# One more seven-product tile in the second FFN, a later start of the down weights in the first, and a down weight made between two copies

## The chip, the cores and the metric

One core of one Trainium2 chip runs the whole layer. The time is device microseconds (us) of one execution, the median over runs. The profile is of one execution, taken by the hardware profiler; its lines name instructions by engine (PE the matrix engine, PEld its weight loads, DVE the vector engine, ACT the scalar engine, POOL and SP the two engines that issue the DMAs here) and by the line of the kernel (L1021).

## The reference

A decoder layer on 512 tokens of width 1024 in float32: a SwiGLU feed-forward block (FFN1), a mixer (attention beside a recurrence), and a second SwiGLU block (FFN2), each between two RMS norms. The change touches the two feed-forward blocks only:

```python
def swiglu(x, w_gate, w_up, w_down):
    return (jax.nn.silu(x @ w_gate) * (x @ w_up)) @ w_down

f = swiglu(rms_norm(h, ffn1_norm_pre[l]), ffn1_w_gate[l], ffn1_w_up[l], ffn1_w_down[l])
h = h + 0.5 * rms_norm(f, ffn1_norm_post[l])
...
f = swiglu(rms_norm(h, ffn2_norm_pre[l]), ffn2_w_gate[l], ffn2_w_up[l], ffn2_w_down[l])
h = h + 0.5 * rms_norm(f, ffn2_norm_post[l])
```

The hidden width is 2816, which is 22 tiles of 128. Weights arrive in float32.

## The kernel before, in words

**Arithmetic.** Every float32 operand is split into a high and a low part (`split`: ACT copies the source to the high part at L269, DVE subtracts that from the source at L270), and a product is three matmuls: high by high, high by low, low by high. A split of 128x1024 is thus one ACT and one DVE instruction, and both engines work nearly all the time to make the operands that PE consumes.

**The hidden tiles of an FFN** are made one after another, in the order that `ffn_order` writes out. The first `NSTD[n]` of them (6 in FFN1, 4 in FFN2) are standard: a gate and an up product, 24 matmuls of 128x512 each. All further tiles are "seven-product" tiles (a Strassen scheme over the two halves of the input width and of the tokens, gate and up sharing products): seven products p1 to p7 of 12 matmuls of 128x256, in the order p1, p5, p6, p2, p7, p3, p4 (`prod`, L994; its matmuls are L1008 to L1010). Their weights are made in `w_forms_in_place` (L646) from one raw load of 1 MB, in four splits that the text calls a (for p1, p2), d (p4), c (p7, p5) and b (p6, p3), with four DVE additions between them (L654, L655, L657, L658). The input must be there in seven forms as well, each one a split (`x_forms` in FFN1, `forms_of` in FFN2, recorded a step at a time after the standard tiles).

Within a seven-product tile, ACT takes the bank of p1 to another bank (L1029, the Y copy; p6 adds to the emptied bank, so it waits for it), then copies the results of p5 and p6 out of their banks (`copy`, L1016: c5 and c6). After p7 a DVE sum (`sum_of`, L1021) forms one half of u from p7's bank and c5. p4 is written into that same bank, so **p4 waits for this sum**. Another sum after p3 forms half of g; two SiLUs and two DVE products (L1049, L1050) end the tile.

**The down projection** is interleaved with the hidden tiles: the first 16 hidden tiles, taken four at a time, are multiplied by their down weights in seven products as well (`step`, L913, 24 matmuls of 128x512 at L922 to L924). They sit in "windows" between a tile's products and its finish. `WINDOWS` gives the steps of four consecutive tiles: p1 and p2, then p5, then p6 and p7, then p3 and p4. In FFN1 the windows of tiles 7 to 12 are written out in `LEAD`. A step's weight is made ahead by `down_form` (L897): a split of 128x1024 from `dr0`, `dr1` or `npair`, SBUF tiles that POOL fills by DMA (L879, or L881 where the load adds to what is there); once made, it issues the load of the next weight into the same place (`supply`, L885), and POOL's DMA waits for the DVE half of the split to be done with the source. The weights that the coming window needs are the tile's `due` list. In the kernel before, all of them are recorded after p2 "behind" the last copy, c6 (`behind("copy")`: in the list order not before it). Tiles with two dues are i = 1, 3 and 4 of each four (p1 and p2; p6 and p7; p3 and p4), tiles with one due are those ahead of p5.

**The start of the down weights.** `begin` (L907) copies one column of `ub` into `dr0` and `dr1` on DVE (L909). The copy reads a hidden tile just made, so the two first POOL loads into `dr0` and `dr1` cannot start before that tile is there: it is a gate in time, and the copied values are overwritten by the loads. `begin` is called after standard tile 1 of each FFN.

**Order.** A scheduler places each engine's instructions in one fixed list at build time, from the recorded order and priorities; each engine then runs its list from top to bottom. Raw weights come through two SBUF buffers, loaded by SP (L215); split weights through four buffers of 128x2x1024.

Of the kernel before, what the change touches and what calls it, by code (L numbers as in the profile page):

```python
# [18 lines left out]
D = 1024  # L19
KC = D // P  # L20
NF = 22
NSTD = {1: 6, 2: 4}
SEVEN = 4
STEPS = ("p1", "p2", "p5", "p6", "p7", "p3", "p4")
WINDOWS = (("p1", "p2"), ("p5",), ("p6", "p7"), ("p3", "p4"))
# [2 lines left out]
LAST = (16, 22)  # L28
# [26 lines left out]
def ffn_order(n):  # L55

    n0 = NSTD[n]
    order = [("std", f) for f in range(n0)]
# [96 lines left out]
def hybrid_layer(ctx: ExitStack, tc: tile.TileContext, xT: bass.AP, xN: bass.AP, wst: bass.AP,  # L155
                 first: bass.AP, rows: bass.AP, wdn: bass.AP, wbig: bass.AP, consts: bass.AP, bias: bass.AP, out: bass.AP):
    nc = tc.nc
    DVE, ACT, PE = nc.vector, nc.scalar, nc.tensor
# [109 lines left out]
    def split(dh, dl, src):  # L268
        ACT.activation(dh, src, AF.Copy)  # L269
        DVE.tensor_sub(dl, src, dh.bitcast(F32))  # L270
# [9 lines left out]
    def tmp(name):  # L280
        return tpool.tile([P, T], F32, name=name, tag="t")
# [534 lines left out]
    def ffn(n, x, r, forms_x, home, pss):  # L816
        t, steps = forms_x
        n0 = NSTD[n]
        ub, wdt, dr = home.ub, home.wd, home.dr
# [50 lines left out]
        def last_act(f):  # L870
            v = home.slot((f - LAST[0] - 1) % 8)
            return v[:, 0, :], v[:, 1, :]
# [12 lines left out]
        def supply(a, p):  # L885

            if p in ("p5", "p6", "p3"):
                dst, qs = home.x, {"p5": ("u0", "u1"), "p6": ("g0",), "p3": ("g1",)}[p]
            else:
                dst, qs = dr[p in ("p2", "p4")], {"p1": ("g0",), "p2": ("g1",), "p7": ("u0", "g0"), "p4": ("u1",)}[p]  # L890
            for i, q in enumerate(qs):
                load(dst, a, q, i > 0 or p in ("p6", "p3"))
            at[p] = dst
# [3 lines left out]
        def down_form(a, p):  # L897
            w = wdt[home.n % 2]
            home.n += 1
            split(w[:, 0, :], w[:, 1, :], at[p])  # L900
            ready[p] = w
            q = NEXT[p]
            a += p in ("p7", "p3", "p4")
            if a < SEVEN:
                supply(a, q)

        def begin():  # L907
            for i in range(2):
                DVE.tensor_copy(dr[i][:, 0:1], ub[:, 1, 0:1])  # L909
            for p in ("p1", "p2"):  # L910
                supply(0, p)

# [73 lines left out]
        @contextmanager  # L986
        def behind(*engines):
            with ExitStack() as es:
                for e in engines:
                    if e in last:  # L990
                        es.enter_context(tc.issue_after(last[e]))
                yield

        def prod(f, w, due):  # L994

            g = tmp("g")
            b, y, z = b_of[f % 2][:, :HB], y_[:, :HB], z_[:, :HB]
            u = ub[:, f % 4, :] if 4 < f < LAST[0] else tmp("u")
            if n == 1 and f in (6, 8):
                u = tmp("u")  # L1000

            def product(p, ps, start):
                if len(t[p][0].shape) == 4:
                    ps = ps.rearrange("q (b t) -> q b t", b=2)
                for k in range(4):
                    ks = slice(k * P, (k + 1) * P)
                    wh, wl, xh, xl = w[p][:, 0, ks], w[p][:, 1, ks], t[p][0][:, k], t[p][1][:, k]
                    PE.matmul(ps, wh, xh, start=start and k == 0, stop=False, skip_group_check=True)  # L1008
                    PE.matmul(ps, wh, xl, start=False, stop=False, skip_group_check=True)  # L1009
                    i = PE.matmul(ps, wl, xh, start=False, stop=k == 3, skip_group_check=True)  # L1010
                last["PE"] = i.ins

            def copy(ps):
                c = tpool.tile([P, HB], F32, name="c", tag="c", bufs=CB)
                with tc.high_priority(offset=EVAC):
                    last["copy"] = ACT.activation(c, ps, AF.Copy).ins  # L1016
                return c

            def sum_of(dst, ps, c):
                with tc.high_priority(offset=EVAC):  # L1020
                    DVE.tensor_add(dst, ps, c)  # L1021

            lead = f == n0
            with behind("PE"):
                product("p1", b, True)
            c1 = copy(b) if lead else None
            if not lead:
                with tc.high_priority(offset=EVAC):
                    ACT.activation(y, b, AF.Copy)  # L1029
            product("p5", z, True)  # L1030
            c5 = copy(z)
            product("p6", b, False)
            c6 = copy(b)
            product("p2", y, lead)
            if lead:
                sum_of(g[:, lo_], y, c1)
            with behind("copy"):
                for a, p in due:
                    down_form(a, p)
            product("p7", b, False)  # L1040
            sum_of(u[:, hi_], b, c5)
            with tc.high_priority(offset=EVAC):
                ACT.activation(g[:, lo_], g[:, lo_] if lead else y, AF.Silu)
            product("p3", z, False)
            sum_of(g[:, hi_], z, c6)
            product("p4", b, False)
            last["ACT"] = ACT.activation(g[:, hi_], g[:, hi_], AF.Silu).ins
            with tc.high_priority(offset=EVAC):
                DVE.scalar_tensor_tensor(u[:, lo_], g[:, lo_], -1.0, b, op0=ALU.mult, op1=ALU.mult)  # L1049
            last["DVE"] = DVE.scalar_tensor_tensor(u[:, hi_], g[:, hi_], -1.0, u[:, hi_], op0=ALU.mult,  # L1050
                                                   op1=ALU.mult).ins
            return u

        def finish(f, u):

            if f >= LAST[0]:
                split(*last_act(f), u)
                if f == LAST[0]:
                    fourth_forms()
            elif n == 1 and f < 10:  # L1060
                if f == 6:
                    second_forms()
                    third_forms()
                    fourth_forms()
                    ACT.activation(ub[:, 0:2, :], late(), AF.Copy)
                    ACT.activation(ub[:, 2, :], u, AF.Copy)
                elif f == 7:
                    first_forms()
                elif f == 8:
                    second_forms()  # L1070
                    third_forms()
                    ACT.activation(ub[:, 0, :], u, AF.Copy)
                elif f == 9:
                    fourth_forms()
            elif f % 4 == 2:
                first_forms()
            elif f % 4 == 3:
                second_forms()
                third_forms()
            elif f % 4 == 0 and f > 4:  # L1080
                fourth_forms()
# [12 lines left out]
        for at_, ev in enumerate(order):  # L1094
            if ev[0] == "std":
                j = ev[1]
                while len(pss) < 2 * j + 2:
                    pss.append(acc_ps())
                    gemm(pss[-1], fetch(keys[len(pss) - 1]), x)
                u = std_out(pss[2 * j], pss[2 * j + 1], j)  # L1100
                if j < len(steps):
                    steps[j]()
                if j == 1:
                    begin()
                if j + 1 == n0:
                    supply(0, "p5")
                    for f in steps[n0:]:
                        f()
                    if n0 > 4:
                        first_forms()  # L1110
            elif ev[0] == "prep":
                with behind("DVE", "ACT"):
                    forms[ev[1]] = w_forms_in_place(("gu", n, ev[1]))
            elif ev[0] == "prod":
                due = order[at_ + 1]
                u = prod(ev[1], forms.pop(ev[1]), [(due[1], p) for p in due[2][:2]] if due[0] == "window" else [])
                if ev[1] == 4:
                    part0(u)
            elif ev[0] == "finish":
                finish(ev[1], u)  # L1120
            else:
                for i, p in enumerate(ev[2]):
                    with behind("PE"):
                        step(ev[1], p)
                    if len(ev[2]) > 2 and i == 0:
                        down_form(ev[1], ev[2][2])
# [56 lines left out]
    with ExitStack() as mx:  # L1183
# [221 lines left out]
        for c in range(0, KC, 2):  # L1405
            g, u = tmp("g"), tmp("u")
# [6 lines left out]
        for i, (c, kind) in enumerate(AHEAD_PAIRS):  # L1413
            g, u = tmp("g"), tmp("u")
# [5 lines left out]
            f = AF.Sigmoid if kind == "sig" else AF.Gelu_apprx_tanh  # L1420
# [7 lines left out]
    with ExitStack() as mx:  # L1428
# [159 lines left out]
        for c in range(KC):  # L1588
# [16 lines left out]
                 {(1, 3): lambda: (bd2.turn(0), bd2.turn(1))})  # L1605
    keys = [(w, 2, i) for i in range(NSTD[2]) for w in ("gate", "up")]
    pss = gemm_first(keys[:NFIRST], u2, [home2.spare()[2]],
# [137 lines left out]
```

## Time and profile before

| | |
|---|---|
| median of 3 runs | 1224.08 us (1223.52 to 1226.09) |
| the profiled execution | 1225.99 us, of which the span of its instructions is 1224.1 us |
| PE busy | 1211.3 us (99%) |
| DVE busy | 979.2 us (80%) |
| ACT busy | 742.8 us (61%) |
| chain of waits that ended last | PE 85%, DVE 8%, DMA 3%, issue 2%, ACT 1% |
| matmuls recorded | 7754 |

A PE row's own duration (0.28 or 0.39 us) overlaps that of the next, since matmuls are pipelined; what counts for the time is the distance from one start to the next. A row of the timeline gives the start in us from the span's beginning, the duration, the engine, the line, the operation, out<-in, the shape, and in brackets the idle time before it with what ended that, where there was any.

### The profile page before, as it was taken

To read this page: it belongs to the slowest core of one execution; us is meant where nothing else is said; L and a number is where in the kernel's file an instruction comes from. 1 tells how busy PE (TensorE), PEld (TensorE's weight loads), DVE (VectorE), ACT (ScalarE), POOL (GpSimd) and SP (SyncE) were. 2 spreads that over 40 slices of the span, in tenths; PEclk is the share of its full clock that TensorE was granted. 3 is DMA by queue.
4 is the path that set the end of the run, shared out by engine and by line. 5 is a ranking of instruction groups with operands and counts; after the bars stand their busy time and mean duration, and the time that the engine had idled before them with its cause. 6 is when DMAs were issued, how large, how long until landed. Compare 5 with 4: busy or idle time off the path is not lost.

```text
span 1224.1 us, 19485 instructions
## 1 busy us (share of the span) xinstructions
PE 1211.3 (99%) x7754; PEld 1100.6 (90%) x7754; DVE 979.2 (80%) x1531; ACT 742.8 (61%) x1232; POOL 84.3 (7%) x139
## 2 busy tenths in 40 slices
PE   9999999999999999999999999999999999999998
PEld 7888989999878899999999888888899999999996
DVE  7899778888579897898776998755689887979864
ACT  6457665655556565665666788634556665656552
POOL 0001101010102000000001000000110010101000
PEclk9999999999999999999999999999999999999999
DMA  7336546464735322222235223524463555555441
GB/s 246 138 104 171 158 111 168 134 165 116 258 134 155 114 94 102 81 79 82 92 138 182 94 86 125 203 83 165 139 199 106 157 158 147 156 139 163 114 155 69
DMA packets 37451, 167.63 MB, mean 137 GB/s; under 512 B 4208, under 2 KB 7664, under 8 KB 25328
## 3 DMA queue, kind: packets, MB, share of 16 engines
q1 hardware_dynamic: 18432, 107.13, 25.3%
q0 software_dynamic: 18928, 59.25, 18.3%
q8 instruction: 61, 1.00, 0.3%
q14 instruction: 30, 0.25, 0.1%
HBM read 153.79 MB, written 8.39 MB: 132 GB/s over the span
## 4 chain that ended last, share of the span: by engine, by line
PE 85%; DVE 8%; DMA 3%; issue 2%; ACT 1%; POOL 0%; SPq 0%; DVEq 0%; ACTq 0%; POOLq 0%
PE bank L1008 9%; PE bank L1009 8%; PE bank L1010 8%; PE bank L675 6%; PE bank L676 6%; PE bank L677 6%; PE bank L284 6%; PE bank L285 6%; PE bank L286 6%; PE bank L923 4%; PE bank L922 4%; PE bank L924 4%; PE bank L405 3%; PE bank L404 3%; PE bank L406 3%
## 5 line engine op out<-in xcount | busy, mean ns | idle before, releaser
L270 DVE TENSOR_TENSOR w<-raw,w 128x1024 fp32r<-128x1024 f32 (+1 forms) x274 | 298.9, 1101 | 63.5 <-ACT w L269 57.8
L269 ACT ACTIVATE w<-raw 128x1024 fp32r<-128x1024 f32 (+1 forms) x274 | 256.8, 956 | 103.1 <-PE bank L286 41.4
L1008 PE MATMUL bank<-big,w 128*128 128x256 f32 x816 | 233.9, 287 | 4.5 <-DVE g L837 1.3
L1009 PE MATMUL bank<-big,w 128*128 128x256 f32 x816 | 230.8, 283 | 0.0
L1010 PE MATMUL bank<-big,w 128*128 128x256 f32 x816 | 229.4, 283 | 0.0
L1008 PEld LDWEIGHTS bank<-big,w 128*128 128x128 f32 x816 | 156.2, 191 | 10.0 <-DVE u L1021 2.0
L1009 PEld LDWEIGHTS bank<-big,w 128*128 128x128 f32 x816 | 156.4, 192 | 1.5
L1010 PEld LDWEIGHTS bank<-big,w 128*128 128x128 f32 x816 | 155.8, 192 | 0.0
L922 PE MATMUL bank<-wd,act 128*128 128x512 f32 x224 | 87.8, 392 | 0.0
L923 PE MATMUL bank<-wd,act 128*128 128x512 f32 x224 | 87.8, 392 | 0.0
L924 PE MATMUL bank<-wd,act 128*128 128x512 f32 x224 | 87.2, 389 | 0.0
L675 PE MATMUL bank<-big,w 128*128 128x256 f32 x252 | 73.0, 290 | 0.0
L677 PE MATMUL bank<-big,w 128*128 128x256 f32 x252 | 71.5, 284 | 0.0
L676 PE MATMUL bank<-big,w 128*128 128x256 f32 x252 | 71.2, 283 | 0.0
L285 PE MATMUL bank<-act,w 128*128 128x512 f32 (+1 forms) x184 | 64.8, 353 | 0.1
L286 PE MATMUL bank<-act,w 128*128 128x512 f32 (+1 forms) x184 | 64.7, 352 | 0.0
L284 PE MATMUL bank<-act,w 128*128 128x512 f32 (+1 forms) x184 | 64.5, 355 | 0.2 <-ACT act L361 0.2
L1016 ACT ACTIVATE c<-bank 128x256 f32<-128x256 f32 x70 | 26.7, 383 | 61.1 <-PE bank L1010 60.7
L270 DVE TENSOR_TENSOR wd<-npair,wd 128x1024 fp32r<-128x1024 f32 x24 | 29.4, 1224 | 39.2 <-ACT wd L269 39.2
L284 PE MATMUL bank<-big,w 128*128 128x512 f32 x144 | 56.0, 389 | 0.0
L285 PE MATMUL bank<-big,w 128*128 128x512 f32 x144 | 56.0, 389 | 0.0
L286 PE MATMUL bank<-big,w 128*128 128x512 f32 x144 | 56.0, 389 | 0.0
(399 smaller groups left out, 3206.3 us busy)
## 6 DMA issues: line engine op xcount, KB each, us to landing
raw<-in_w SPq DMA_DIRECT2D x90, 1024.0 KB, 5.0
dr<-in_wdn POOLq DMA_DIRECT2D x40, 512.0 KB, 5.2
npair<-in_wdn POOLq DMA_DIRECT2D x32, 512.0 KB, 5.5
big<-act POOLq DMA_DIRECT2D x6, 512.0 KB, 3.8
h<-in_x SPq DMA_DIRECT2D x8, 256.0 KB, 5.2
h<-in_xn POOLq DMA_DIRECT2D x4, 512.0 KB, 5.2
raw<-in_wbig SPq DMA_DIRECT2D x2, 1024.0 KB, 4.8
kept_m<-h POOLq DMA_DIRECT2D x4, 512.0 KB, 2.9
```

The costliest lines, as they stand in the source:

```text
L269: ACT.activation(dh, src, AF.Copy)
L270: DVE.tensor_sub(dl, src, dh.bitcast(F32))
L284: PE.matmul(ps, wh, xh, start=first, stop=False)
L285: PE.matmul(ps, wh, xl, start=False, stop=False)
L286: PE.matmul(ps, wl, xh, start=False, stop=last)
L675: PE.matmul(ps, wh, xh, start=start and k == 0, stop=False, skip_group_check=True)
L676: PE.matmul(ps, wh, xl, start=False, stop=False, skip_group_check=True)
L677: PE.matmul(ps, wl, xh, start=False, stop=k == 3, skip_group_check=True)
L922: PE.matmul(ps, xh, wh, start=start and k == 0, stop=False, skip_group_check=True)
L1008: PE.matmul(ps, wh, xh, start=start and k == 0, stop=False, skip_group_check=True)
L1009: PE.matmul(ps, wh, xl, start=False, stop=False, skip_group_check=True)
L1010: i = PE.matmul(ps, wl, xh, start=False, stop=k == 3, skip_group_check=True)
```

## The change

Three edits.

1. `NSTD[2]` goes from 4 to 3: hidden tile 3 of FFN2 becomes a seven-product tile. Its u goes to `ub[:, 3]` like that of the standard tiles before it, and `finish` makes no forms at tile 3 (`part0` at tile 4 makes all of them, as before). The steps that make the input's forms and the start of the p5 down weight follow standard tile 2 in place of tile 3.
2. `begin` takes the tile: in FFN1 it is called after standard tile 2 and reads `ub[:, 2]`; in FFN2 it stays after tile 1.
3. In `prod`, all dues but the last are recorded after c5, behind it, so between c5 and c6; only the last stays behind c6. Nothing changes in tiles with one due. This holds in both FFNs.

```diff
-NSTD = {1: 6, 2: 4}
+NSTD = {1: 6, 2: 3}
...
-        def begin():
+        def begin(j):
             for i in range(2):
-                DVE.tensor_copy(dr[i][:, 0:1], ub[:, 1, 0:1])
+                DVE.tensor_copy(dr[i][:, 0:1], ub[:, j, 0:1])
...
-            u = ub[:, f % 4, :] if 4 < f < LAST[0] else tmp("u")
+            u = ub[:, f % 4, :] if 4 < f < LAST[0] or f < 4 else tmp("u")
...
             product("p5", z, True)
             c5 = copy(z)
+            with behind("copy"):
+                for a, p in due[:len(due) - 1]:
+                    down_form(a, p)
             product("p6", b, False)
             c6 = copy(b)
...
             with behind("copy"):
-                for a, p in due:
+                for a, p in due[len(due) - 1:]:
                     down_form(a, p)
...
-            elif f % 4 == 3:
+            elif f % 4 == 3 and f > 4:
...
-                if j == 1:
-                    begin()
+                if j == (2 if n == 1 else 1):
+                    begin(j)
```

Where the instructions go. First DVE near the start of FFN1, before the change; `h`, `t1`, `t2` and `big` belong to the input's forms, `w8` are weight splits, L837 to L840 are the ends of standard tiles, L909 is the gate:

```order
L523 TENSOR_TENSOR t1_325<-h_93 128x1024
L909 COPY dr0_100<-ub_97 128x1
L909 COPY dr1_101<-ub_97 128x1
L270 TENSOR_TENSOR w8_471<-raw_469,w8_471 128x1024
L270 TENSOR_TENSOR w8_498<-raw_469,w8_498 128x1024
L837 TENSOR_TENSOR g_387<-bank4_77,npair_95 128x512
L839 TENSOR_TENSOR ub_97<-bank0_73,npair_95 128x512
```

And after it, further on in the same list:

```order
L839 TENSOR_TENSOR ub_97<-bank0_73,npair_95 128x512
L527 SCALAR_TENSOR_TENSOR t2_388<-h_94,t1_325 128x1024
L840 TENSOR_TENSOR ub_97<-ub_97,g_383 128x512
L270 TENSOR_TENSOR big_390<-t1_325,big_390 128x1024
L541 TENSOR_TENSOR h_93<-h_94,h_93 128x4x256
L909 COPY dr0_100<-ub_97 128x1
L909 COPY dr1_101<-ub_97 128x1
L270 TENSOR_TENSOR w8_536<-raw_534,w8_536 128x1024
```

The two copies moved eight rows down; the rows between them are otherwise in the same order.

Second, DVE in FFN2, tile 7, which has two dues (`wd1` from `npair` for p6, `wd0` from `dr0` for p7). Before:

```order
L658 TENSOR_TENSOR raw_9180<-raw_9180 128x512
L270 TENSOR_TENSOR wd1_7929<-npair_95,wd1_7929 128x1024
L270 TENSOR_TENSOR wd0_7928<-dr0_7930,wd0_7928 128x1024
L1021 TENSOR_TENSOR ub_7927<-bank1_74,c_9224 128x256
L270 TENSOR_TENSOR w8_9184<-raw_9180,w8_9184 128x1024
L1021 TENSOR_TENSOR g_9198<-bank5_78,c_9238 128x256
```

After:

```order
L658 TENSOR_TENSOR raw_9235<-raw_9235 128x512
L270 TENSOR_TENSOR wd1_7929<-npair_95,wd1_7929 128x1024
L270 TENSOR_TENSOR wd0_7928<-dr0_7930,wd0_7928 128x1024
L270 TENSOR_TENSOR w8_9239<-raw_9235,w8_9239 128x1024
L1021 TENSOR_TENSOR ub_7927<-bank1_74,c_9279 128x256
L270 TENSOR_TENSOR w8_9238<-raw_9235,w8_9238 128x1024
```

The split c of the next tile's weights now stands ahead of the sum for which p4 waits. The same swap stands in tiles 8, 9, 10, 13, 15, 17, 19 and 20 of FFN1 and in tiles 8, 9, 11, 13, 15, 17, 19 and 20 of FFN2. Tiles with one due had the order w8, then sum, before the change already.

Third, ACT in FFN1, tile 11 (window p6 and p7). Before:

```order
L934 ACTIVATE s5_873<-bank7_80 128x512
L1029 ACTIVATE bank2_75<-bank1_74 128x256
L1016 ACTIVATE c_1469<-bank1_74 128x256
L269 ACTIVATE w8_1415<-raw_1411 128x1024
L269 ACTIVATE wd0_98<-npair_95 128x1024
```

After:

```order
L934 ACTIVATE s5_873<-bank7_80 128x512
L269 ACTIVATE wd0_98<-npair_95 128x1024
L1029 ACTIVATE bank2_75<-bank1_74 128x256
L1016 ACTIVATE c_1472<-bank1_74 128x256
L269 ACTIVATE w8_1415<-raw_1411 128x1024
```

The first due, made from `npair`, moved ahead of the Y copy, of c6 and of a weight split; c5 stands some rows further up in both lists.

## The prediction

> **What bounds the kernel now.** I read the page's busy shares first, then its chain of waits, then what PE waits for, then timelines at the places that the change touches.
>
> ```profile
> PE 1211.3 (99%) x7754; PEld 1100.6 (90%) x7754; DVE 979.2 (80%) x1531; ACT 742.8 (61%) x1232; POOL 84.3 (7%) x139
> PE 85%; DVE 8%; DMA 3%; issue 2%; ACT 1%; POOL 0%; SPq 0%; DVEq 0%; ACTq 0%; POOLq 0%
> ```
>
> PE is the bound. A change can win by giving PE less to do, or by taking away one of the few places where PE stands. It can lose by making new ones. The waits of PE in FFN1's tiles (60 to 330 us) are these:
>
> ```profile
> PE bank L1008 <- ACT c L1016: 1.5, 3, 0.5
> PE bank L1008 <- DVE g L837: 1.3, 1, 1.3
> PE bank L1008 <- DVE u L1021: 1.3, 2, 0.9
> PE bank L1008 <- DVE ub L1021: 0.2, 1, 0.2
> ```
>
> That is 4.3 us of idle time in all, and the same view of FFN2 (900 to 1210 us) names none. The profiled execution took 1225.99 us, 1.9 more than its span and 1.9 more than the median of 1224.08. I sum against its rows and put the result on the median.
>
> **Edit 1, one more seven-product tile: -0.80 us on PE.** The prices are the distances between starts, from a stretch of standard products and from a whole seven-product tile:
>
> ```profile
> 908.21 0.40 PE L284 MATMUL bank<-act,w 128*128 128x512 f32 x1
> ...
> 924.56 0.28 PE L1008 MATMUL bank<-big,w 128*128 128x256 f32 x1
> ...
> 979.31 0.28 PE L1008 MATMUL bank<-big,w 128*128 128x256 f32 x1
> ...
> 989.48 0.40 PE L922 MATMUL bank<-wd,act 128*128 128x512 f32 x1
> ```
>
> Three standard products, 72 matmuls of 128x512, take 16.35 us: 0.227 each. The seven-product tile, 84 matmuls of 128x256, takes 10.17, of which 0.10 is the usual small gap ahead of p4: 0.120 each. A standard tile is 48 x 0.227 = 10.88, the other 84 x 0.120 = 10.08. The difference is 0.80 us.
>
> [...]
>
> What edit 1 costs is cover. The input's forms, the first tile's weights and the second tile's are made while PE runs standard products:
>
> ```profile
> 908.20:924.60 16.40, 16.40 (x75) 13.57 (x74) 13.28 (x18) 6.88 (x9) 1.09 (x2) 1.00 0.40 136
> 915.55 1.06 ACT L269 ACTIVATE big<-ts 128x1024 fp32r<-128x1024 f32 x1 [3.10 <-DVE ts L616]
> ```
>
> In that stretch DVE is busy 13.28 of 16.40 us, and the last form (for p4) is split only at 915.55, after DVE's L616. The change leaves one standard product there in place of three: PE reaches p1 at 908.21 + 5.45 = 913.66, p6 after p1 and p5 (2 x 12 x 0.120) at 916.54, p4 near 922.3. Moving the rows of DVE and ACT up in their new order, I find c1 done near 916.05, behind that form and a weight split on ACT, and the sum ahead of p4 near 922.25. So all is just in time, with 0.1 to 0.5 us to spare. I take 0. The far bound is +2, two DVE splits of 1.2 that come out of step; below 0 nothing can come, since PE does not stand there now.
>
> **Edit 2, the later gate: -2.95 us.** What happens at the gate, in rows of DVE, POOL, the load that SP issues at 44.27 (issue to landing 8.5 us) and the one that it issues at 56.81 (4.7), then ACT and DVE:
>
> ```profile
> 41.75 0.22 DVE L909 COPY dr<-ub 128x1 f32<-128x1 f32 x2
> 42.24 1.20 POOL L881 DMA_DIRECT2D dr<-in_wdn  x2 [41.79 <-DVE dr L909]
> raw<-in_w SPq DMA_DIRECT2D x1, 1024.0 KB, 8.5
> raw<-in_w SPq DMA_DIRECT2D x1, 1024.0 KB, 4.7
> 52.81 0.63 ACT L269 ACTIVATE w<-raw 128x512 fp32r<-128x512 f32 x1 [5.15 <-DMA raw<-in_w]
> 54.43 1.23 DVE L270 TENSOR_TENSOR big<-h,big 128x1024 fp32r<-128x1024 f32 x1 [3.18 <-ACT big L269]
> 54.40:82.00 27.60, 25.71 (x143) 22.16 (x142) 27.57 (x38) 14.47 (x22) 0.53 (x1) 1.00 0.30 96
> ```
>
> The two down weights start their loads right before the raw weights of tile 6, and this load takes 8.5 us in place of 4.7. ACT stands 5.15 us for it, with a form queued behind, and DVE stands 3.18 for that form. DVE is then busy for 27.57 of the next 27.60 us, and at the end of that stretch PE stands three times:
>
> ```profile
> 71.66 0.39 PE L286 MATMUL bank<-act,w 128*128 128x512 f32 x1
> 73.39 0.36 PE L1008 MATMUL bank<-big,w 128*128 128x256 f32 x1 [1.34 <-DVE g L837]
> 77.04 0.38 PE L1008 MATMUL bank<-tx,w 128*128 128x256 f32 x1 [0.55 <-ACT c L1016]
> 83.45 0.39 PE L1008 MATMUL bank<-big,w 128*128 128x256 f32 x1 [0.40 <-DVE u L1021]
> ```
>
> The first start is 1.73 after the one ahead of it, 1.50 over the cadence, of which 1.34 is idle time by its bracket. The three brackets sum to 2.29; with that extra 0.16 at each (0.48), and some 0.1 more at the matmul behind a restart (I read 0.22 there where 0.12 is usual), it is 3.0 us in all. The new gate stands behind L541, some 8 us on. The load then lands near 49.0, ACT's split and its form go at once, and DVE's full stretch begins about 3.2 us sooner; a backlog that starts 3.2 us sooner hands everything to PE in time. Late next would be the weight buffers, which PE frees in its own time, but later than DVE is ready by under 0.5 us. So -2.95 with a little left over. The bounds are -3.1 and -1. The loads that are moved go to 50 to 55 us on POOL's queue, beside the next raw load (4.7 now); if that one stretches to 8.5 as well, it lands near 62, about when the 61.55 of before does. The two weights themselves are wanted by the first window, in tile 7, behind all three waits above, so they have some 30 us.
>
> **Edit 3, the split dues.** Three kinds of place.
>
> (a) *The usual tiles.* First DVE at the end of FFN2's tile 6, with one due, and of tile 7, with two; behind that PE at the same places, where p4 starts at 959.40 and 972.31:
>
> ```profile
> 957.79 1.23 DVE L270 TENSOR_TENSOR w<-raw,w 128x1024 fp32r<-128x1024 f32 x1 [0.21 <-ACT w L269]
> 958.93 0.42 DVE L1021 TENSOR_TENSOR ub<-bank,c 128x256 f32<-128x256 f32 x1
> ...
> 970.70 1.22 DVE L270 TENSOR_TENSOR wd<-dr,wd 128x1024 fp32r<-128x1024 f32 x1
> 971.84 0.42 DVE L1021 TENSOR_TENSOR ub<-bank,c 128x256 f32<-128x256 f32 x1
> ```
>
> ```profile
> 958.98 0.28 PE L1010 MATMUL bank<-big,w 128*128 128x256 f32 x1
> 959.40 0.39 PE L1008 MATMUL bank<-big,w 128*128 128x256 f32 x1
> ...
> 972.31 0.38 PE L1008 MATMUL bank<-big,w 128*128 128x256 f32 x1
> ```
>
> With one due the split c of the next weights goes ahead of the sum, the sum ends at 959.35, and p4 starts 0.42 after its forerunner: 0.30 late. With two, the second due takes that time and the sum comes at once. The change makes the first due earlier, which empties DVE's place ahead of the sum, and the list puts split c there: every such tile now has the tail of the one-due tile. That is +0.30 each in FFN1's tiles 9, 10 and 15 and FFN2's 7, 8, 9, 11, 13 and 15: nine, +2.7 us. Tile 13 of FFN1 has such a wait already; in 17, 19 and 20 ACT makes c early enough. Where both dues still go ahead of the sum (tile 16 of FFN1, 12 and 16 of FFN2) I take +0.2 each, +0.6; the bounds are 0 and 0.7, the length of a short DVE row.
>
> (b) *Tiles 7 and 8 of FFN1.* Here PE stands for c5 (another of the three c rows) and for the sum (the 0.9 in the waits). With edit 3 c5 comes ahead of the window's rows on ACT and its wait goes, but the early due of tile 8 waits for its load much as in (c), and the list has split c ahead of the sum here too: -0.35 net, between -1 and +0.3.
>
> (c) *Tile 11 of FFN1.* POOL's load of its first due, that load's time to landing, then ACT's Y copy, PE's p6 and ACT's split of that due:
>
> ```profile
> 155.44 0.86 POOL L879 DMA_DIRECT2D npair<-in_wdn  x1 [6.20 <-DVE wd L270]
> npair<-in_wdn POOLq DMA_DIRECT2D x1, 512.0 KB, 5.5
> 159.56 0.37 ACT L1029 ACTIVATE bank<-bank 128x256 f32<-128x256 f32 x1 [0.54 <-PE bank L1010]
> 159.98 0.39 PE L1008 MATMUL bank<-tx,w 128*128 128x256 f32 x1
> 162.95 1.05 ACT L269 ACTIVATE wd<-npair 128x1024 fp32r<-128x1024 f32 x1
> ```
>
> The weight lands at 155.44 + 5.5 = 160.9. Before, ACT makes it at 162.95, after Y. Now it stands ahead of Y, so ACT waits for the load to 160.9, splits to 161.95 and does Y until 162.3. p6 starts there in place of 159.98: +2.35. Queued behind are c6, the b weight split and the SiLU, all later than before, and PE waits for c6 through p7. Some comes back: PE's delay gives DVE time, and the wait for c5 in tile 12 (one of the three c rows of the waits, 0.5 idle and 0.7 over the cadence) and part of one behind it go. Net +1.4, between +0.8 and +2.5. [...] If ACT could pass the waiting split, (c) would be -0.7 in place of +1.4. [...]
>
> **The sum:** -0.80 - 2.95 + 2.7 + 0.6 - 0.35 + 1.4 = +0.6. On the median this is 1224.08 + 0.6 = **1224.7 us**: the gate's gain is spent on edit 3.
>
> **The rivals.**
>
> *A, edit 3 costs little.* The list's rows end in time because the first due is out of the way sooner, so (a) is 0.1 a tile at most, and the load in (c) lands earlier, since p5's weight is made sooner in tile 10. For it: ACT is busy only 61%. Against it: the one-due tail is measured. It gives 1224.1 - 3.75 + 0.6 = 1220.9, and 1218 if the stalls of (b) go altogether. Chance 0.20.
>
> *B, the cover in FFN2 is gone (slower).* ACT's copy c1 and Y are queued behind the p4 form, which waits for DVE's L616, and DVE has 13.28 us of work for a stretch now 10.9 shorter. From the point where that form ends after 916.5, p6 waits, and every product behind it. Two DVE splits late and c1 behind them are +2.4, with (c) in full +1.0 more: 1224.7 + 3.4 = 1228.1. Chance 0.28.
>
> *C, the later gate does nothing,* since the raw load only collides with the two others later, or the weight buffers hold DVE's stretch where it is: +2 of the 2.95 back, 1226.7, on the edge of no change. Its chance is inside those of the forecast and of B.
>
> **Chances and range.** The forecast has 0.52. No change is within 0.2%, 2.45 us, about what a measurement of this kernel can tell: 1221.6 to 1226.5. Faster by more 0.20, within 0.52, slower by more 0.28. The range takes in A's and B's times but for their tails: 1220.5 to 1229.
>
> **What would show it.** Edit 1: 36 more matmuls than before, one standard product (5.45 us) between FFN2's last input form on PE and tile 3's p1, and no PE wait up to tile 5; waits for c or `big` there speak for B. Edit 2: no 5.15 us wait on ACT and no 3.18 on DVE near 52, and no PE wait between 70 and 84. Edit 3: PE waits for `ub` of L1021, 0.2 each in nine tiles; one wait for the ACT bank of L1029 near 157, of about 2 us. Without these waits the sum is wrong by up to 4, and A is right.

## The result, and the profile after

The changed kernel takes 1230.2 us (median of 5 runs, 1228.83 to 1231.36) beside 1223.82 us (1223.45 to 1226.09) for the kernel before: a ratio of 1.0048, 95% interval 1.0038 to 1.0059. It is **6.4 us slower**, where no change was forecast (+0.6) and the range ended at 1229. Its profiled execution took 1231.18 us.

The page of the changed kernel, busy time and chain:

```profile
PE 1211.9 (99%) x7790; PEld 1102.1 (90%) x7790; DVE 988.7 (80%) x1540; ACT 749.8 (61%) x1238; POOL 84.5 (7%) x139
PE 77%; DVE 12%; ACT 5%; issue 3%; DMA 2%; SPq 0%; DVEq 0%; ACTq 0%
```

36 matmuls more, as expected, and the busy time of PE says nothing of the loss. The chain does: 12% through DVE in place of 8, 5% through ACT in place of 1. What PE waits for in FFN1 (60 to 330 us), and then from the end of the mixer on (870 to 1215 us):

```profile
PE bank L1008 <- ACT bank L1029: 2.2, 1, 2.2
PE bank L1008 <- ACT c L1016: 1.6, 2, 1.4
PE bank L1008 <- DVE u L1021: 1.1, 1, 1.1
PE bank L1008 <- DVE ub L1021: 0.2, 1, 0.2
```

```profile
PE bank L491 <- DVE u L483: 1.4, 1, 1.4
```

The wait for L837 (1.3 before) is gone; the repeated profile of the kernel before, further down, has none either. New are one for the Y copy (L1029), which was forecast, a long one for a copy (L1016), and one ahead of FFN2 for L483, which nothing in the prediction speaks of. The many waits of 0.3 us at p4 do not appear: of the 0.42 us between two starts there (974.92 and 975.34 below), 0.28 is the row of the matmul ahead, whose end is modelled, so this view undercounts. I therefore use a second measure, worked out from PE's rows: the distance from each start to the next, less 0.2267 us for a 128x512 matmul, 0.120 for 128x256 and 0.111 for 128x128, summed by stretch. In us lost, for profiled executions of the kernel before (as in the prediction, and once more), of kernels with one edit, and of the changed one:

| stretch | before | before, again | edit 1 alone | edit 2 alone | edit 3 alone | changed |
|---|---|---|---|---|---|---|
| start to tile 6 of FFN1 | 4.34 | 2.55 | 3.42 | 2.66 | 2.71 | 3.10 |
| FFN1 tile 6 | 1.52 | 1.08 | 1.52 | 0.17 | 1.44 | 0.18 |
| tiles 7 and 8 | 2.26 | 2.39 | 2.25 | 2.26 | 2.28 | 3.98 |
| tiles 11 and 12 | 2.22 | 2.20 | 2.22 | 2.25 | 5.37 | 4.08 |
| tiles 9, 10, 13 to 20 | 1.83 | 1.72 | 1.55 | 1.55 | 3.07 | 3.07 |
| tile 21 to the start of FFN2's tiles | 10.42 | 10.67 | 12.01 | 10.16 | 10.29 | 11.81 |
| FFN2 up to tile 5 | 0.31 | 0.31 | 0.21 | 0.31 | 0.30 | 0.21 |
| FFN2 tiles 6 to 21 | 2.70 | 2.63 | 3.32 | 2.66 | 4.90 | 4.90 |
| sum | 25.60 | 23.56 | 26.49 | 22.03 | 30.36 | 31.32 |

From the repeated profile of before to the changed kernel this is 31.32 - 23.56 = +7.76, less 0.80 for the cheaper tile: +6.96, and the two spans differ by 1229.0 - 1222.1 = 6.9.

**The gate (edit 2), as forecast in kind.** The load of tile 6's weights, ACT's first instruction that needs it, and the step from the last standard matmul to tile 6, in the changed kernel:

```profile
raw<-in_w SPq DMA_DIRECT2D x1, 1024.0 KB, 4.7
49.35 0.63 ACT L269 ACTIVATE w<-raw 128x512 fp32r<-128x512 f32 x1 [1.37 <-DMA raw<-in_w]
71.92 0.39 PE L286 MATMUL bank<-act,w 128*128 128x512 f32 x1
72.14 0.28 PE L1008 MATMUL bank<-big,w 128*128 128x256 f32 x1
```

The load takes 4.7 us, ACT waits 1.37 in place of 5.15, and tile 6 begins 0.22 us after the matmul ahead of it, with no wait.

**The usual tiles (edit 3), as forecast in kind and size.** FFN2's tile 7 in the changed kernel, DVE and then PE:

```profile
972.28 1.23 DVE L270 TENSOR_TENSOR wd<-dr,wd 128x1024 fp32r<-128x1024 f32 x1 [0.21 <-ACT wd L269]
973.72 1.23 DVE L270 TENSOR_TENSOR w<-raw,w 128x1024 fp32r<-128x1024 f32 x1 [0.22 <-ACT w L269]
974.87 0.42 DVE L1021 TENSOR_TENSOR ub<-bank,c 128x256 f32<-128x256 f32 x1
```

```profile
974.92 0.28 PE L1010 MATMUL bank<-big,w 128*128 128x256 f32 x1
975.34 0.39 PE L1008 MATMUL bank<-big,w 128*128 128x256 f32 x1
```

Split c (973.72) runs ahead of the sum, and p4 starts 0.42 after its forerunner, 0.30 over the cadence: the tail of the one-due tile.

**Tile 11 of FFN1, as forecast in kind.** ACT, then PE:

```profile
160.73 1.06 ACT L269 ACTIVATE wd<-npair 128x1024 fp32r<-128x1024 f32 x1 [2.08 <-DMA npair<-in_wdn]
161.69 0.37 ACT L1029 ACTIVATE bank<-bank 128x256 f32<-128x256 f32 x1
162.11 0.39 PE L1008 MATMUL bank<-tx,w 128*128 128x256 f32 x1 [2.24 <-ACT bank L1029]
```

ACT waits for the load with Y behind it, and p6 starts 2.40 late (159.59 to 162.11, less 0.12); 2.35 was forecast.

**Not forecast: ahead of FFN2.** ACT and DVE where the last token block of the mixer is normed, then PE's transpose of that block:

```profile
889.11 0.63 ACT L269 ACTIVATE w<-raw 128x512 fp32r<-128x512 f32 x1 [4.18 <-DMA raw<-in_w]
889.65 1.04 ACT L478 ACTIVATE facc<-h 128x1024 f32<-128x1024 f32 x1
893.37 1.41 DVE L483 SCALAR_TENSOR_TENSOR u<-h,stat,ub 128x512 f32<-128x512 f32 x2
894.26 0.30 PE L491 MATMUL bank<-cst,u 128*128 128x128 f32 x1 [1.41 <-DVE u L483]
```

ACT stands 4.18 us for a raw load with the square of that token block (L478) queued behind. The order of ACT's rows says why. The kernel before has no weight split between L383 and L478 here, and the square comes right after DVE's L475:

```profile
882.40 0.29 ACT L383 ACTIVATE stat<-stat 128x1 f32<-128x1 f32 x1
885.54 1.06 ACT L478 ACTIVATE facc<-h 128x1024 f32<-128x1024 f32 x1 [2.84 <-DVE h L475]
```

In the changed kernel ACT's row ahead of the split at 889.11 is that L383:

```profile
884.63 0.29 ACT L383 ACTIVATE stat<-stat 128x1 f32<-128x1 f32 x1
```

So the split, d of FFN2's tile 3, now stands between the two. With three standard tiles in place of four, the raw load under way at that moment is the one for the first seven-product tile. Its split d goes to one of the two small buffers (`w4`), which are free there, while its larger splits wait for `w8` buffers; as I read it, the scheduler, for which weight splits have priority, puts it as early as it can.

### The profile page after: what moved, and what is told of

The parts are those of the page before. It is cut to its first block, busy times and chain, and to the rows that moved or that the text cites. A ratio compares the mean times of both kernels' runs of the same rounds, so it can differ in the third digit from the quotient of the medians.

```text
span 1229.0 us, 19583 instructions
## 1 busy us (share of the span) xinstructions
PE 1211.9 (99%) x7790; PEld 1102.1 (90%) x7790; DVE 988.7 (80%) x1540; ACT 749.8 (61%) x1238; POOL 84.5 (7%) x139
## 4 chain that ended last, share of the span: by engine, by line
PE 77%; DVE 12%; ACT 5%; issue 3%; DMA 2%; SPq 0%; DVEq 0%; ACTq 0%
PE bank L1008 8%; PE bank L1009 8%; PE bank L1010 8%; PE bank L675 6%; PE bank L676 6%; PE bank L677 6%; PE bank L922 4%; PE bank L923 4%; PE bank L924 4%; DVE w L270 4%; PE bank L285 3%; PE bank L286 3%; PE bank L284 3%; PE bank L406 3%; PE bank L404 3%
## 5 line engine op out<-in xcount | busy, mean ns | idle before, releaser
L269 ACT ACTIVATE w<-raw 128x1024 fp32r<-128x1024 f32 (+1 forms) x276 | 261.2, 957 | 107.9 <-PE bank L286 39.2
L1008 PE MATMUL bank<-big,w 128*128 128x256 f32 x840 | 240.8, 287 | 5.2 <-ACT c L1016 1.6
L1009 PE MATMUL bank<-big,w 128*128 128x256 f32 x840 | 237.4, 283 | 0.0
L1010 PE MATMUL bank<-big,w 128*128 128x256 f32 x840 | 237.4, 283 | 0.0
L1008 PEld LDWEIGHTS bank<-big,w 128*128 128x128 f32 x840 | 160.8, 191 | 12.1 <-DVE ub L1021 5.7
L1009 PEld LDWEIGHTS bank<-big,w 128*128 128x128 f32 x840 | 161.0, 192 | 1.4
L1010 PEld LDWEIGHTS bank<-big,w 128*128 128x128 f32 x840 | 160.9, 192 | 0.1
L675 PE MATMUL bank<-big,w 128*128 128x256 f32 x252 | 73.0, 290 | 0.0
L677 PE MATMUL bank<-big,w 128*128 128x256 f32 x252 | 71.5, 284 | 0.0
L676 PE MATMUL bank<-big,w 128*128 128x256 f32 x252 | 71.2, 283 | 0.0
L285 PE MATMUL bank<-act,w 128*128 128x512 f32 (+1 forms) x168 | 58.6, 349 | 0.3 <-DVE act L362 0.3
L286 PE MATMUL bank<-act,w 128*128 128x512 f32 (+1 forms) x168 | 58.5, 349 | 0.0
L284 PE MATMUL bank<-act,w 128*128 128x512 f32 (+1 forms) x168 | 58.4, 352 | 0.0
L1016 ACT ACTIVATE c<-bank 128x256 f32<-128x256 f32 x72 | 27.6, 383 | 43.7 <-PE bank L1010 42.1
```

Source lines behind the costliest of these rows:

```text
L284: PE.matmul(ps, wh, xh, start=first, stop=False)
L285: PE.matmul(ps, wh, xl, start=False, stop=False)
L286: PE.matmul(ps, wl, xh, start=False, stop=last)
```

## The experiments

Each was timed beside the kernel before on the same chip; the ratios have 95% intervals.

**Each edit alone, and edits 1 and 2 together.** Edit 2 alone (`only_gate`):

```diff
...
-                if j == 1:
-                    begin()
+                if j == (2 if n == 1 else 1):
+                    begin(j)
```

> Only edit 2, the gate after standard tile 2 of FFN1. Theory: the three PE waits between 71 and 84 us go (-2.85), and about 0.5 comes back in tile 8, where the down weight's load is not as much earlier as PE is: -2.4, about 1221.4 us. Rival: the earlier PE only meets the same loads later and gives all of it back in tiles 7 to 12: 1223.8 us.

Measured 1222.8 us beside 1224.19, 0.9991 (0.9982 to 1.0): -1.4, half of the price forecast, in an interval that just reaches zero. The waits at tile 6 are gone, and nothing came back in tiles 7 to 12 (2.26 and 2.25, as before). So neither theory nor rival: the gain was smaller to begin with.

Edit 1 alone (`only_tile`):

```diff
-NSTD = {1: 6, 2: 4}
+NSTD = {1: 6, 2: 3}
...
```

> Only edit 1, the seven-product tile 3 in FFN2. Theory: -0.80 for the cheaper tile, +1.5 to +1.8 for a new wait of PE ahead of FFN2 (near 890 us), where ACT stands for a raw load with the square of token block 3 queued behind: +0.7 to +1.0, about 1224.7 us, and the wait is in the trace. Rival: that wait in the changed kernel comes from the shift by the other edits or from chance, and is absent here: 1223.0 us.

Measured 1225.04 beside 1224.19, 1.0011 (1.0002 to 1.002): +0.85, and the wait ahead of FFN2 is there. The seven-product tile brings its 0.80 and costs about 1.6. In the table the stretch ahead of FFN2 holds 1.3 to 1.6 of new loss, and in this execution tile 13 of FFN2 loses 0.7 more than before.

Edit 3 alone (`only_dues`):

```diff
             c5 = copy(z)
+            with behind("copy"):
+                for a, p in due[:len(due) - 1]:
+                    down_form(a, p)
...
-                for a, p in due:
+                for a, p in due[len(due) - 1:]:
```

> Only edit 3, the first of two dues between c5 and c6. Theory: +0.30 in nine usual tiles, +0.3 in tile 19 of each FFN, +1.9 in tiles 11 and 12 of FFN1, and between -0.4 and 0 in tiles 7 and 8 (PE is 2.8 us later there than with the later gate, so the load is in time for c6): +4.8, about 1228.6 us. Rival: edit 3 is as dear in tile 8 alone as together with the gate (+1.7 there): 1230.5 us.

Measured 1230.64 beside 1224.19, 1.0054 (1.004 to 1.0068): +6.4, as much as the whole change. Tiles 7 and 8 lose no more than before (2.28), so that part of the theory holds; tiles 11 and 12 lose 3.2 us more than before, where 1.9 was expected. What adds to the wait there is PE's clock. In edit 3 alone, with PEclk behind the counts:

```profile
159.00:161.20 2.20, 0.02 (x1) 0.00 (x0) 0.24 (x1) 1.33 (x2) 0.00 (x0) 1.00 0.06 11
161.20:162.50 1.30, 1.25 (x10) 1.25 (x11) 0.99 (x1) 0.00 (x1) 0.00 (x0) 1.00 0.00 0
162.50:165.90 3.40, 3.40 (x18) 3.40 (x18) 1.78 (x3) 2.42 (x4) 0.85 (x1) 0.51 0.54 75
165.90:170.00 4.10, 4.10 (x36) 4.10 (x35) 3.65 (x5) 2.52 (x4) 0.56 (x1) 0.99 0.63 148
```

PE idles for 2.2 us, runs at full clock for 1.3, and then at half clock for 3.4 us: 18 matmuls in a time in which 28 fit. Sixteen starts are 0.09 late each, which is 1.4 us beyond the wait. In the changed kernel's profiled execution the clock stayed at 1.00 behind the same wait (162.10 to 165.50, 28 matmuls).

Edits 1 and 2 (`gate_tile`):

> Edits 1 and 2 without edit 3. Theory, as the sum of the two alone: -2.4 + 0.8, about 1222.2 us, with the wait near 890 us in the trace and no row of PE that waits 2 us in tile 11. Rival: edit 3 is not what makes the changed kernel slow, and this one is slow too, above 1226 us.

Measured 1223.92 beside 1224.19, 1.0 (0.9991 to 1.0009); -0.3, where the two alone sum to -0.54. Without edit 3 no gain or loss can be told from zero.

**The wait ahead of FFN2** (`all_forms_later`). The changed kernel, with those weight forms behind the first SiLU of FFN2 (`prep` already stands behind `last["ACT"]`):

```diff
-                ACT.activation(g, psg, AF.Silu)
+                i = ACT.activation(g, psg, AF.Silu)
+                if f == 0:
+                    last["ACT"] = i.ins
```

> The changed kernel, with the weight forms of FFN2's first seven-product tile held behind the first SiLU of FFN2, so that ACT squares token block 3 before it waits for those weights. Theory: the PE wait near 892 us goes, -1.6 from the changed kernel: 1228.6 us. Rival: block 3 is late for another reason and the wait stays, 1230.2 us, or it moves to tile 3, whose weights are now later.

Measured 1228.73 beside 1224.12, 1.0033 (1.0021 to 1.0046): -1.5 from the changed kernel, about as expected. ACT there:

```profile
887.49 1.06 ACT L478 ACTIVATE facc<-h 128x1024 f32<-128x1024 f32 x1 [2.83 <-DVE h L475]
```

The square waits for DVE alone, and PE has no wait for L483. Tile 3 of FFN2 loses 0.18, as in the changed kernel, so its weights had time to spare. In tile 11 this execution has the half clock too (0.50 from 161.00 to 163.70, 14 matmuls).

**Tiles 8 and 11** (`all_but_8_11`). The changed kernel, but these two keep the old place of both dues:

```diff
+            cut = len(due) - 1 if n == 2 or f not in (8, 11) else 0
...
-                for a, p in due[:len(due) - 1]:
+                for a, p in due[:max(cut, 0)]:
...
-                for a, p in due[len(due) - 1:]:
+                for a, p in due[max(cut, 0):]:
```

> The changed kernel, but tiles 8 and 11 of FFN1 keep both dues behind c6. Theory: there ACT waits for a load with a copy queued behind, so the waits for the Y copy of tile 11 (2.4) and for c6 of tile 8 (1.5) go, and about 0.8 of the old small ones come back: -3, about 1227.2 us. Rival: the load is late anyway and PE waits as long at the sums and copies behind: above 1229.5 us.

Measured 1226.78 beside 1224.12, 1.0021 (1.0012 to 1.003): -3.4. Tile 11 still waits 1.2 us for its sum and tile 13 has a new wait of 1.8 for its own. The gain is near the expected 3; whether a part of the old wait moved on to tile 13 is not shown.

**Whether it is the load or the queue behind it** (`all_behind_y`). The changed kernel, with the first due behind Y too:

```diff
-                    ACT.activation(y, b, AF.Copy)
+                    last["y"] = ACT.activation(y, b, AF.Copy).ins
...
-            with behind("copy"):
+            with behind("copy", "y"):
                 for a, p in due[:len(due) - 1]:
```

> The changed kernel, with the first due behind the Y copy as well as c5 (ACT's list in tile 11 of FFN1 then reads Y, due, c6; all other tiles as before). Theory: it is not the late load that costs 2.4 us in tile 11 but the Y copy queued behind it; with Y ahead the wait for the bank of L1029 goes, -2.2 to -2.6 from the changed kernel's 1230.2, and -1.5 more in the executions in which TensorE's granted clock falls after that wait: about 1227.2 us. Rival: the load holds up c6 and the sum instead, and PE waits as long two products later: 1229.5 us or more.

Measured 1227.8 beside 1224.37, 1.0029 (1.0019 to 1.0039): -2.4. ACT in tile 11, then PE at p6 and at p4:

```profile
156.96 0.37 ACT L1029 ACTIVATE bank<-bank 128x256 f32<-128x256 f32 x1 [0.54 <-PE bank L1010]
158.28 1.06 ACT L269 ACTIVATE wd<-npair 128x1024 fp32r<-128x1024 f32 x1 [0.95 <-DMA npair<-in_wdn]
```

```profile
157.38 0.39 PE L1008 MATMUL bank<-tx,w 128*128 128x256 f32 x1
163.54 0.39 PE L1008 MATMUL bank<-big,w 128*128 128x256 f32 x1 [1.34 <-DVE ub L1021]
```

ACT still waits for the same load, now with nothing behind it that p6 needs, and p6 has no wait. So the queue cost p6 its 2.4 us, not the late load. The rival has a share: the sum ahead of p4 is now 1.5 late, so tiles 11 and 12 together fall from 4.08 only to 2.53, beside 2.20 in the kernel before. That the run gains 2.4 as well is chance: tiles 11 and 12 give 1.55, and 1.8 more between the two profiles is tiles 7 and 8 (3.98 and 2.18), where other executions with edit 3 lose 2.3 or 2.4 too. PE's longest wait is 1.4 us here, and the clock stays at 1.00.

**Split c ahead of the sum** (`all_sum_first`). The changed kernel; split c and what follows it in `w_forms_in_place` is recorded behind the sum (here `s_u`), DVE's half held to it:

```diff
-            sum_of(u[:, hi_], b, c5)
+            s_u = sum_of(u[:, hi_], b, c5)
+            for rest in later:
+                rest(s_u)
...
+        def rest(after=None):
+            with ExitStack() as es:
+                es.enter_context(tc.high_priority(offset=AHEAD))
+                ACT.activation(c[:, 0, :], raw[:, 0:1024], AF.Copy)
+                if after is not None:
+                    es.enter_context(tc.issue_after(after))
+                DVE.tensor_sub(c[:, 1, :], raw[:, 0:1024], c[:, 0, :].bitcast(F32))
```

> The changed kernel, with DVE's half of split c of the next tile held behind the sum that p4 waits for (from tile 8 on in FFN1, 6 in FFN2). Theory: the 0.30 us wait of p4 in 16 tiles is DVE's order alone and goes: -4.8, about 1225.4 us, with no DVE ub wait of L1021 left there. Rival: the sum is bound by the bank or c5, and the waits stay: 1230.2 us; or c comes too late for the next tile: above that.

Measured 1222.61 beside 1224.12, 0.9987 (0.9978 to 0.9996): 7.6 us faster than the changed kernel. FFN2's tile 7 on DVE (split c is at L663 in this kernel, the sum at L1033), and PE at p4:

```profile
966.39 1.23 DVE L270 TENSOR_TENSOR wd<-dr,wd 128x1024 fp32r<-128x1024 f32 x1 [0.22 <-ACT wd L269]
967.91 0.43 DVE L1033 TENSOR_TENSOR ub<-bank,c 128x256 f32<-128x256 f32 x1 [0.29 <-PE bank L1022]
968.25 1.22 DVE L663 TENSOR_TENSOR w<-raw,w 128x1024 fp32r<-128x1024 f32 x1
```

```profile
968.31 0.28 PE L1022 MATMUL bank<-big,w 128*128 128x256 f32 x1
968.43 0.28 PE L1020 MATMUL bank<-big,w 128*128 128x256 f32 x1
```

DVE now waits for p7's bank, not the reverse, and PE goes from p3 to p4 without a gap. A usual tile loses -0.01 over its own 84 matmuls in place of 0.39: the small 0.10 ahead of p4, which I had taken for the tile's own, goes with the 0.30. Not everywhere: tile 16 of each FFN and tile 12 of FFN2, which had no such wait, now lose 0.38 at the same place. In the rows of the table, tiles 9, 10, 13 to 20 and FFN2's 6 to 21 lose 2.25 in place of 7.97, so -5.7 where -4.8 was expected; tiles 7 and 8, 1.03 in place of 3.98, give most of the rest, and a part of that is the changed kernel's own late load of tile 8.

The same hold in the kernel before, without any edit (`base_sum_first`):

> The kernel before with only the sum held ahead of split c. Theory: 0.39 in each of six one-due tiles and about 0.09 in each of sixteen others go, -3.5: about 1220.7 us, which would say that p4's waits on this sum cost the kernel before more than any of the three edits could bring. Rival: split c comes late for the next tile and gives it back: 1224 us.

Measured 1223.15 beside 1224.37, 0.9993 (0.9984 to 1.0002): -1.2, a third of what was expected, in an interval that takes in zero. The one-due tiles fall from 0.39 to -0.01, but the two-due ones keep 0.09: there both dues stand ahead of the sum, and the second of them ends too late. And tiles 11 and 12 lose 0.3 more (2.48). Edit 3 alone costs 6.4, and the hold takes that away; but with both, beside edits 1 and 2, the gain over the kernel before is 1.5, of which `gate_tile` had 0.3 and the hold alone has 1.2. So up to here the hold makes the early first due harmless, and does not yet make it pay.

**Putting it together.** Edits 1 and 2 with the held forms and the sum first (`best`):

> Edits 1 and 2 with the held weight forms and the sum ahead of split c, without edit 3. Theory: 1224.2 - 1.4 (gate) - 0.8 (tile) - 0.3 each in six tiles with one due: about 1220.2 us, faster than both kernels. Rival: the gains do not add up because the next late operand takes their place: 1222 us or more.

Measured 1221.91 beside 1224.12, 0.9978 (0.997 to 0.9987): -2.2, where -3.9 was expected; tiles 7 and 8 (2.67) and 11 and 12 (2.47) keep their waits, and FFN2's tile 13 loses 1.07, where the kernel before loses 0.1 to 0.2. All three edits with all three repairs (`best2`):

> All three edits with the three repairs (first due behind Y, the held weight forms of FFN2's first tile, the sum ahead of split c). Theory, from the changed kernel with the sum first (1222.6): -1.6 for the wait near 892, -1.5 for the bank wait of tile 11: about 1219.5 us. Rival: the repairs uncover the next waits (c6 of tiles 8 and 11, the sums where two dues stand ahead), 1221.9 us or more, as the version without edit 3.

Measured **1218.62 us** beside 1224.37, 0.9955 (0.9942 to 0.9967): the fastest of all, 5.7 us faster than the kernel before and 11.6 faster than the changed one. It differs from `best` only in the early first due, held behind Y, so here edit 3 pays: 3.5 us. Its waits of PE from 60 to 1215 us are two:

```profile
PE bank L284 <- DVE facc L1595: 0.4, 1, 0.4
PE bank L1022 <- DVE ub L1035: 0.2, 1, 0.2
```

**The kernel before once more** (`before_again`):

> The kernel before, unchanged, profiled once more. Theory: the 1.50 us wait ahead of tile 6 at 71.66, and a raw load of 8.5 us ahead of it, belong to the first profiled execution, which was 1.8 us above the median; here the load takes about 7.2 us and the waits of tiles 5 and 6 sum to about 1.4 us. Rival: the 1.50 us wait is there again, and the later gate should have brought 2.9 us.

Measured 1224.16 beside 1224.37, 0.9998 (0.9988 to 1.0008); its profiled execution took 1223.94 us, 2.0 less than that of the prediction. The same raw load, and the step to tile 6:

```profile
raw<-in_w SPq DMA_DIRECT2D x1, 1024.0 KB, 6.7
71.37 0.39 PE L286 MATMUL bank<-act,w 128*128 128x512 f32 x1
71.60 0.28 PE L1008 MATMUL bank<-big,w 128*128 128x256 f32 x1
```

The load takes 6.7 us, not 8.5, and the wait of 1.50 us ahead of tile 6 is not there. Nor is it in the executions of edits 1 and 3 alone, whose lists are the same up to here. Tile 6 itself loses 1.08.

## Why the prediction was wrong

The forecast was +0.6 and the result +6.4. Three steps failed: the gate's price was read from one execution with a wait that the others lack, the 0 for the cover of edit 1 was looked for at one end only, and the price of (c) was too low. Point by point:

- **Edit 1's price, right.** -0.80 from the cadence, and the cover behind it holds: tile 3 loses 0.18 and FFN2 up to tile 5 loses 0.21 in all, 0.31 before. Rival B, the lost cover, did not come.
- **Edit 1's other end, missed.** The step that failed is "I take 0" for the cover, with its search for trouble from 908 us on, at the new tile's start, only. Taking out a standard tile moves the seven-product tile's load and split d ahead of the end of the mixer too, and ACT's list has it before the last square: +1.5 (`all_forms_later`). The list was there to be read; I followed it from FFN2's start on, and the move is ahead of that. The far bound of +2 covers the size by luck: it stood for two DVE splits out of step, which did not come.
- **Edit 2's price, mis-sized.** -2.95 in the forecast, -1.4 measured. The mechanism is right: the load, 8.5 and 6.7 us in the two profiles of the kernel before, takes 4.7 in the changed kernel; ACT's wait for it, 5.15, 3.92 and 3.71 us with the old gate (the kernel before, `only_tile`, `only_dues`), is 1.37, 1.32 and 1.42 with the new one (the changed kernel, `only_gate`, `gate_tile`); and tile 6, which lost 1.1 to 1.5 us, loses 0.17 or 0.18 in eight of the nine kernels with the later gate. In `gate_tile` it still loses 1.19, though ACT waits only those 1.42; why is not shown. But 1.5 us of the 2.95 was the wait behind 71.66, which only the first profiled execution had. That execution was 1.9 us above the median, and the prediction said so, and then took the whole gain from the median. About half of what it took out was that excess.
- **Edit 3 (a), right.** +3.3 was forecast. Tiles 9, 10, 13 to 20 of FFN1 lose 1.35 and tiles 6 to 21 of FFN2 2.27 more than in the repeated profile: +3.6. The tail of the one-due tile came as read. Tile 19 of each FFN has it too (0.3), where I expected none, and tiles with two dues ahead of the sum have none (-0.01), where I allowed 0.2.
- **Edit 3 (b), about 0 in the usual case, inside its bounds.** -0.35 forecast. Edit 3 alone loses 2.28, and `all_forms_later` and `all_behind_y` lose 2.38 and 2.18, beside 2.26 and 2.39 in the two profiles of the kernel before. The changed kernel's profiled execution lost 3.98, since there c6 was queued behind the split of tile 8, whose load landed late (ACT waits 2.79 us for it, and PE 1.35 for c6): the mechanism of (c), which the prediction named there and gave no price of its own.
- **Edit 3 (c), right in its wait and mis-sized in the net.** The wait is 2.40 (2.35 forecast). The net is +1.9 at full clock, +3.0 and +3.2 where the clock falls, against +1.4 with an upper bound of 2.5. What failed is the part that was to come back, too high by about 0.5, and the bound: it had no term for a PE that comes back slower than it left. Of the three executions with this wait of 2.2 us, two have the half clock (`only_dues`, `all_forms_later`).

No one step carries the miss. The gate fell short by 1.5, the wait ahead of FFN2 adds 1.5, (c) about 1.1, and (a) and (b) about 0.3 each. With -1.4 for the gate, +1.5 ahead of FFN2 and +2.5 for (c), which is between its values at the two clocks, the same sum gives -0.8 - 1.4 + 1.5 + 3.6 + 0 + 2.5 = +5.4 of the 6.4 measured; the rest is of the size of the differences between executions.

What stays open: how often the clock falls in the changed kernel, since its own profile shows none; and why the load of tile 8's first due took 7.3 us in the changed kernel's profiled execution, where the same load takes 5.4 in the kernel before.

## What to carry to other kernels

When the profiled execution is above the median, look for the wait that makes it so before any gain is subtracted from the median. In tile 11 ACT kept the order of its list: while it stood 2.08 us for a load, the Y copy stood behind it, and p6 started 2.40 us late; with Y ahead, p6 had no wait (`all_behind_y`). So an instruction that waits for a load may only be moved up past work that nobody waits for: the test is not whether the load is late, but who stands behind it. And freeing a place ahead of an urgent instruction is worth nothing if the scheduler may fill it: hold the filler explicitly, and keep the early due behind the copy that PE waits for, then it pays (3.5 us here).

## What the runs showed of the hardware

PE's granted clock fell to half after a wait of 2.2 us, in two of the three executions with such a wait. In `only_dues` it reads 0.51 from 162.50 to 165.90, 1.3 us behind the restart. In `all_forms_later` it reads 0.50 right at the restart, from 160.60 on (p6 is at L1010 to L1012 there):

```profile
160.69 0.58 PE L1010 MATMUL bank<-tx,w 128*128 128x256 f32 x1 [2.15 <-ACT bank L1031]
161.07 0.42 PE L1011 MATMUL bank<-tx,w 128*128 128x256 f32 x1
161.29 0.41 PE L1012 MATMUL bank<-tx,w 128*128 128x256 f32 x1
```

The starts are 0.22 apart in place of 0.12. So this wait of PE had a second price, 1.4 us in `only_dues`, that a sum of waits leaves out. In the third execution, the changed kernel's, the clock stays at 1.00 behind a wait of 2.24 us. In all the others the longest wait of PE from 60 to 330 and from 870 to 1215 us is 1.7 us (`only_tile`), and the granted clock reads 1.00 in every stretch read from 60 to 320 and from 880 to 1215 us. What decides whether the clock falls is not shown.
